# Moving the block inverses' transfers to GpSimd's queue in a hybrid decoder layer, with new transfer prices in the planner

## The chip, the core and the metric

The kernel runs on one core of one Trainium2 chip. The core has a matrix engine (TensorE, PE in the profile), a vector engine (VectorE, DVE), a scalar engine (ScalarE, ACT), a general engine (GpSimd, POOL) and a queue engine (SyncE, SP) that issues transfers. Each takes its own instructions in order and waits on semaphores for the others. Transfers between DRAM and the on-chip memory (SBUF) are issued by SP, ACT or POOL and carried out by 16 transfer engines. The metric is the device time in microseconds (us), the median of several executions; the profile is of one further execution.

## The reference

One layer of a decoder, with a residual and a last norm, in float32 (1024 tokens, width 2048):

```python
h = rmsnorm(x, ln_g);  proj = h @ w_in                     # 2048 x 6672
g_u, g_v, g_z, d_q, d_k, d_v, d_z, d_a, d_b, c_q, c_z = split(proj)
out_a = gmlp_spatial_gating(g_u, g_v, ...) * silu(g_z)     # 4 groups of 128, chunks of 128
q, k, v = split(causal_conv_silu(concat(d_q, d_k, d_v)))   # 8 heads of 128
o = gated_delta_rule(l2norm(q), l2norm(k), v, g, beta)
out_b = rmsnorm(o, dn_norm_g) * silu(d_z)
out_c = softmax(c_q @ mk.T / sqrt(128)) @ mv * silu(c_z)   # 256 memory tokens, 4 heads
y = rmsnorm(x + concat(out_a, out_b, out_c) @ w_out, final_g)
```

The delta rule solves, in every chunk and head, a triangular system with a unit diagonal, T = (I + A)^-1, where A holds the decayed products of the keys. That inverse is what the change is about.

## The kernel before, in words

Products in full precision are made from float32 split into a high and a low part: ACT makes the high part (a cast: `whi`, `ahi`, `zh`), DVE the low one (a subtraction: `wlo`, `alo`, `zl`), and PE adds three products. So each operand that comes from DRAM goes transfer, cast, subtraction, matmul. The large products use a seven-product scheme over 2 x 2 blocks (`seven`): a step takes two left and two right blocks of 128 x 512 and makes 24 matmuls of 512 columns. Three buffers hold raw left operands and three hold split ones, and likewise for the right side.

The delta rule's heads come in pairs. `front` makes a pair's keys, queries and products `gt` (128 x 1024) for one half of the tokens. `blocks_out` (L958) cuts the 32 x 32 blocks of the diagonal out of `gt` and stores them to DRAM (`gdr`), four transfers a pair, each of 256 runs of 128 bytes. When four pairs are there, `inverse` (L971) loads them (`gd`, one block per partition), with 16 transfers from POOL, and inverts all blocks at once by 31 elimination steps on DVE (62 operations, interleaved with other work). It stores the inverses `ti` (to `tdr`) and their transposes `gd` (to `udr`). `levels` (L999) later loads these 32 x 32 blocks into `tblk` and `ut`, 12 transfers of SP a pair, and builds 128 x 128 inverses from them by small matmuls, before `back` runs the scan over the chunks. This happens twice: "early" for heads 0 to 3, whose scan runs beside the first large products, and "late" for heads 4 to 7.

Before the change ACT's queue issues the stores of `gdr` (32 in all) and of `tdr` and `udr` (four each per inverse, 128 KB each); POOL issues the loads of `gd`. POOL also does the masks of the decay matrices, the small powers of the norms, and memsets.

The order of everything is written by a planner (`Plan`, L54). It records all operations with what they depend on, gives each a price, and runs a list schedule: every engine takes, of the operations that are ready, the one with the lowest rank and then the earliest in the program. `issue` (L223) then emits the operations sorted by planned time. Each engine's order in the built program is thus a consequence of the prices. For transfers the prices are the issue time on the queue, a share of a common pipe (bytes over 300 per ns, at least 512 bytes a row), a fixed latency of 1600 ns, and additions for some shapes. ACT's transfers have a pipe of their own at half the rate.

All operations are recorded through one helper, so nearly every row of the profile has the line L292 (the emitting loop); tiles tell them apart. In the built program a transfer of SP or ACT takes the next of eight semaphores, and waits for the one that used it before; POOL's transfers have eight others.

Of the kernel before, what the change touches and what calls it, by code (L numbers as in the profile page):

```python
# [44 lines left out]


class Op:
    __slots__ = ("eng", "fn", "args", "kw", "cls", "idx", "cost", "lat", "nbytes", "lock", "n", "succ", "ready", "at",
                 "lead", "tail", "table")


# [9 lines left out]
class Plan:  # L61
    SEEN = {"pe": 55.0, "act": 35.0, "dve": 35.0, "pool": 78.0, "sp": 60.0}
    SLACK = 600.0
    OVERLAP = {"pe": 0.0, "act": 90.0, "dve": 80.0, "pool": 50.0, "sp": 0.0}
    DMA_RATE = 300.0
    DMA_FIXED = 1600.0
    SWITCH = 250.0
    TABLES = {AF.Exp: "exp", AF.Silu: "silu", AF.Gelu_apprx_tanh: "gelu"}
    TABLE_LOAD = 1500.0
# [113 lines left out]
    def price(self, o, name, outs, ins):  # L183

        out = outs[0]
        n = math.prod(out.shape[1:])
        both = [*outs, *ins]
        psum = any(i.space == PSUM for i in both)
        pointer = any(i.shape[-1] == 1 and math.prod(i.shape[1:]) == 1 for i in ins[1:])
        o.nbytes = o.lock = 0  # L190
        o.lat = 0.0
        if name == "dma_start":
            o.cost = {"sp": 380.0, "act": 430.0, "pool": 1000.0}[o.eng]
            rows = math.prod(out.shape[:-1])
            o.nbytes = max(4 * math.prod(out.shape), 512 * rows)
            src = ins[0]
            pieces = src.shape[-1] < 128 or out.shape[-1] < 128
            if out.space == DRAM:
                o.lat = 9000.0 if out.shape == (32, 8, 32) else 3000.0
            elif pieces or out.shape[0] < 32:  # L200
                o.lat = 2400.0
            elif list(src.ap)[0][0] == 0:
                o.lat = 4000.0
        elif o.eng == "pe":
            passes = 1 if ins[0].dtype == F32R else 2 if name == "transpose" else 4
            o.cost = max(13.3 + n / 2.4 * passes, 222.0 if passes == 4 else 110.0) if out.shape[0] == P else 30.0
            o.lat = 175.0
        elif o.eng == "act":
            o.cost = (165.0 if psum else 200.0) + 0.82 * n + (105.0 if pointer else 0.0)
            o.cost += 190.0 if "accum_out" in o.kw else 0.0  # L210
        elif o.eng == "dve":
            n = max([n] + [math.prod(i.shape[1:]) for i in ins])
            o.cost = (n + 151) / 0.96 + (60.0 if pointer and name == "scalar_tensor_tensor" else 0.0)
            o.lock = not psum and (name.startswith("tensor_") or name == "scalar_tensor_tensor")
            o.lock = o.lock and name != "tensor_reduce"
        else:
            o.lock = 1
            if name in ("memset", "affine_select"):
                o.cost = 100.0 + 0.83 * n * (1 if name == "memset" else 1.4)
                o.lat = 800.0 if name == "affine_select" else 0.0  # L220
            else:
                o.cost = 750.0 + 150.0 * (n - 1) if n < 8 else 200.0 + 2.1 * n

    def issue(self):
        free = dict.fromkeys(self.SEEN, 0.0)
        soon = {e: [] for e in free}
        now = {e: [] for e in free}
        held = {"dve": 0.0, "pool": 0.0}
        dma = beside = 0.0
        table = "exp"  # L230
        for o in self.ops:
            if o.n == 0 and o.lead is o:
                heapq.heappush(soon[o.eng], (0.0, o.idx))
        left = len(self.ops)
        while left:
            best = None
            for e in free:
                if now[e]:
                    t = free[e]
                elif soon[e]:  # L240
                    t = max(free[e], soon[e][0][0])
                else:
                    continue
                if best is None or t < best[0]:
                    best = (t, e)
            t, e = best
            while soon[e] and soon[e][0][0] <= t:
                i = heapq.heappop(soon[e])[1]
                heapq.heappush(now[e], (self.ops[i].cls, i))
            if e == "act":  # L250
                other = [(c + self.STAY * (self.ops[i].table not in (None, table)), i, c) for c, i in now[e]]
                _, i, c = min(other)
                now[e].remove((c, i))
                heapq.heapify(now[e])
                head = self.ops[i]
            else:
                head = self.ops[heapq.heappop(now[e])[1]]
            for o in (head, *head.tail):
                t = max(t, free[e])
                if o.table not in (None, table):  # L260
                    t, table = t + self.TABLE_LOAD, o.table
                o.at = t
                left -= 1
                if o.lock:
                    t = max(t, held["pool" if e == "dve" else "dve"])
                end = t + o.cost
                if o.lock:
                    held[e] = end
                free[e] = end - min(self.OVERLAP[e], 0.5 * o.cost)
                done = end + o.lat  # L270
                if o.nbytes and e == "act":
                    beside = max(beside, end) + 2 * o.nbytes / self.DMA_RATE
                    done = beside + self.DMA_FIXED + o.lat
                elif o.nbytes:
                    dma = max(dma, end) + o.nbytes / self.DMA_RATE
                    done = dma + self.DMA_FIXED + o.lat
                for s in o.succ:
                    if s.eng != e or o.nbytes:
                        when = done + self.SEEN[s.eng] + (self.SLACK if s.eng == "pe" else 0.0)
                    elif e == "pe":  # L280
                        when = free[e]
                    else:
                        when = end + 34.0
                    s.ready = max(s.ready, when)
                    s.n -= 1
                    if s.n == 0:
                        heapq.heappush(soon[s.eng], (s.ready, s.idx))
            if len(head.tail) > 7:
                free[e] += self.SWITCH
        self.ops.sort(key=lambda o: (o.at, o.idx))  # L290
        for o in self.ops:
            o.fn(*o.args, **o.kw)  # L292
# [3 lines left out]
def kernel(  # L296
# [35 lines left out]
    def DT(shape, name, dt=F32):  # L332
        return dr.tile(list(shape), dt, name=name, tag=name)[:]
# [624 lines left out]
    def blocks_out(gt, n):  # L958

        gv = gt.rearrange("p h t i -> p (h t) i")  # L960
        gdr = [DT([8, 32, 32], f"gdr{n}_{b}") for b in range(4)]
        for b in range(4):
            sl = slice(b * 32, (b + 1) * 32)
            with rank(1):
                S.dma_start(gdr[b].rearrange("c j i -> j c i"), gv[sl, :, sl])
        return gdr

    def flat(start, *aps):
# [2 lines left out]
    def inverse(gdrs, n, cls):  # L971

        nr = 32 * len(gdrs)
        gd = ring["inv"]()[0:nr].rearrange("p (a b) -> p a b", b=32)
        for i, gdr in enumerate(gdrs):
            for b in range(4):
                with rank(1):
                    flat(G.dma_start, gd[i * 32 + b * 8 : i * 32 + (b + 1) * 8], gdr[b])
        ti = ring["inv"]()[0:nr].rearrange("p (a b) -> p a b", b=32)
        tmp = y1[0:nr].rearrange("p c m -> p (c m)")  # L980
        with rank(4):
            G.memset(ti, 0.0)
            G.affine_select(out=ti, in_=ti, compare_op=ALU.not_equal, fill=1.0, base=0,
                            pattern=[[1, 32], [-1, 32]], channel_multiplier=0)
        with rank(cls):
            for j in range(31):
                n1, m = 31 - j, j + 1
                tv = tmp[:, 0 : n1 * m].rearrange("p (n m) -> p n m", m=m)
                V.tensor_tensor(out=tv, in0=bc(gd[:, j, j + 1 :], m), in1=rep(ti[:, j, 0:m], n1), op=ALU.mult)
                V.tensor_tensor(out=ti[:, j + 1 :, 0:m], in0=ti[:, j + 1 :, 0:m], in1=tv, op=ALU.add)  # L990
            V.tensor_copy(gd.rearrange("p i m -> p m i"), ti)
        tdr, udr = ([DT([32, 32, 32], f"{t}{n}_{i}") for i in range(len(gdrs))] for t in ("tdr", "udr"))
        for i in range(len(gdrs)):
            with rank(1):
                flat(S.dma_start, tdr[i], ti[i * 32 : (i + 1) * 32])
                flat(S.dma_start, udr[i], gd[i * 32 : (i + 1) * 32])
        return list(zip(tdr, udr))

    def levels(gt, tdr, udr):  # L999

# [771 lines left out]
```

## Time and profile before

| | us |
|---|---|
| median of 3 executions | 1661.45 (1657.06 to 1662.36) |
| profiled execution | 1662.46 |
| its span, first to last instruction | 1660.7 |

The page lists, for each engine, busy time and share of the span. The list of waits names, for an engine, what ended its idle time, the sum, how often, and the longest. In a timeline a row is start, duration, engine, operation, output and inputs, count, and in brackets the idle time ahead of it and what ended it; ACTq, SPq and POOLq are issues of transfers. The row of a window gives the stretch, its length, the busy time of PE, PE's weight loads, DVE, ACT and POOL, the granted clock of PE as a share of full speed, the busy share of the transfer engines, and GB/s. A tile's row gives the shortest, median and longest duration in ns, and "to landing" the time from a transfer's issue to its arrival.

### The profile page before, as it was taken

How to read it: one execution, taken by the hardware profiler on the slowest of the kernel's cores; microseconds unless marked ns; L12 is line 12 of the kernel's file. 1: busy time of each engine (PE TensorE's matmuls, PEld its weight loads, DVE VectorE, ACT ScalarE, POOL GpSimd, SP SyncE). 2: the span in 40 equal slices, each digit the busy share in tenths (PEclk: the TensorE clock that was granted, in tenths of full speed). 3: DMA queues.
4: the chain of work that ended last, by engine and by line, in shares of the span. 5: the costliest groups of instructions: out<-in, count | busy, mean ns of one | idle time of the engine just before them, and what ended most of it. 6: DMA issues, size and time to landing. Idle time of an engine off the chain costs nothing.

```text
span 1660.7 us, 26037 instructions
## 1 busy us (share of the span) xinstructions
PE 1623.1 (98%) x8570; PEld 1357.9 (82%) x8570; DVE 1253.7 (75%) x2081; ACT 1027.4 (62%) x2226; POOL 109.2 (7%) x166
## 2 busy tenths in 40 slices
PE   8999999999899999999999998999999999999997
PEld 7888888887788888878887886888888878788886
DVE  4865777778666567989998885777768887688875
ACT  5957765765275556987775345776666774345445
POOL 0000100130000000100013000000000000000001
PEclk9999999999999999999999999999999999999999
DMA  7887888797888886599878977788968769679746
GB/s 253 241 235 222 256 288 244 231 311 269 280 270 263 283 273 201 192 283 337 294 250 274 303 230 205 232 263 305 312 209 291 264 220 353 202 251 307 227 140 241
DMA packets 320625, 427.88 MB, mean 258 GB/s; under 512 B 58669, under 2 KB 139238, under 8 KB 320490
## 3 DMA queue, kind: packets, MB, share of 16 engines
q1 hardware_dynamic: 308290, 418.87, 77.6%
q10 hardware_dynamic: 10088, 4.21, 1.0%
q0 software_dynamic: 2112, 3.15, 0.7%
q8 instruction: 67, 1.10, 0.3%
q14 instruction: 68, 0.56, 0.1%
HBM read 338.52 MB, written 87.06 MB: 256 GB/s over the span
## 4 chain that ended last, share of the span: by engine, by line
PE 82%; DMA 7%; DVE 5%; ACT 2%; issue 2%; SPq 0%; ACTq 0%; DVEq 0%; POOLq 0%; POOL 0%
PE acc L292 62%; PE dn L292 21%; DMA wraw<-in_w_in_dram 2%; DVE wlo L292 1%; DMA wraw<-hTd 1%; DMA wraw<-in_w_out_dram 1%; DVE alo L292 1%; ACT whi L292 1%; DMA y<-in_w_in_dram 1%; DVE y L292 0%; SPq L292 0%; ACTq L292 0%; DMA hTd<-tn 0%; ACT ahi L292 0%; DVE wraw L292 0%
## 5 line engine op out<-in xcount | busy, mean ns | idle before, releaser
L292 PE MATMUL acc<-ahi,whi 128*128 128x512 f32 (+1 forms) x1152 | 451.0, 392 | 1.2 <-ACT whi L292 0.9
L292 PE MATMUL acc<-alo,whi 128*128 128x512 f32 (+1 forms) x1152 | 451.0, 392 | 0.0
L292 PE MATMUL acc<-ahi,wlo 128*128 128x512 f32 (+1 forms) x1152 | 450.3, 391 | 0.2 <-DVE wlo L292 0.2
L292 PEld LDWEIGHTS acc<-ahi,whi 128*128 128x128 f32 x1152 | 217.3, 189 | 43.4 <-ACT whi L292 1.3
L292 PEld LDWEIGHTS acc<-ahi,wlo 128*128 128x128 f32 x1152 | 217.2, 189 | 41.5 <-DVE wlo L292 0.8
L292 PEld LDWEIGHTS acc<-alo,whi 128*128 128x128 f32 x1152 | 217.1, 188 | 40.7
L292 PE MATMUL acc<-ahi,zh 128*128 128x512 f32 x736 | 237.1, 399 | 6.0 <-DVE y L292 5.0
L292 DVE TENSOR_TENSOR wlo<-wraw,whi 128x512 fp32r<-128x512 f32 (+1 forms) x170 | 157.3, 926 | 73.9 <-ACT whi L292 64.5
L292 ACT CAST whi<-wraw 128x512 fp32r<-128x512 f32 (+1 forms) x170 | 137.3, 808 | 121.8 <-PE acc L292 69.1
L292 DVE TENSOR_TENSOR alo<-raws,ahi 128x1024 fp32r<-128x1024 f32 x131 | 159.7, 1220 | 51.0 <-ACT ahi L292 48.3
L292 ACT CAST ahi<-raws 128x1024 fp32r<-128x1024 f32 x131 | 137.4, 1049 | 62.2 <-PE dn L292 28.2
L292 PEld LDWEIGHTS acc<-ahi,zh 128*128 128x128 f32 x736 | 138.7, 191 | 33.9 <-ACT whi L292 5.4
L292 PE MATMUL acc<-ahi,zl 128*128 128x512 f32 x368 | 146.3, 397 | 0.0
L292 DVE TENSOR_TENSOR ahi<-y,ahi 128x1024 fp32r<-128x1024 f32 x65 | 79.2, 1218 | 34.6 <-ACT ahi L292 24.2
L292 ACT CAST ahi<-y 128x1024 fp32r<-128x1024 f32 x65 | 68.1, 1048 | 45.2 <-PE acc L292 20.3
L292 PEld LDWEIGHTS acc<-ahi,zl 128*128 128x128 f32 x368 | 70.1, 190 | 13.7
L292 ACT CAST zh<-wraw 128x1024 fp32r<-128x1024 f32 x36 | 37.8, 1050 | 42.2 <-PE acc L292 25.2
L292 DVE TENSOR_TENSOR zl<-wraw,zh 128x1024 fp32r<-128x1024 f32 x36 | 43.9, 1220 | 21.5 <-ACT zh L292 21.3
L292 PE MATMUL dn<-wlo,ahi 128*128 128x512 f32 x152 | 59.0, 389 | 0.0
L292 PE MATMUL dn<-whi,alo 128*128 128x512 f32 x152 | 59.0, 389 | 0.0
L292 PE MATMUL dn<-whi,ahi 128*128 128x512 f32 x152 | 58.8, 389 | 0.0
L292 POOL TENSOR_TENSOR small<-small,mhalf 128x1 f32<-128x1 f32 x26 | 17.1, 662 | 627.7 <-DVE small L292 627.7
(387 smaller groups left out, 3105.0 us busy)
## 6 DMA issues: line engine op xcount, KB each, us to landing
wraw<-in_w_in_dram SPq DMA_DIRECT2D x268, 256.0 KB, 4.4
raws<-sd SPq DMA_DIRECT2D x148, 256.0 KB, 4.0
y<-in_w_in_dram SPq DMA_DIRECT2D x92, 256.0 KB, 4.7
y<-sd SPq DMA_DIRECT2D x77, 256.0 KB, 4.7
wraw<-in_w_out_dram SPq DMA_DIRECT2D x64, 256.0 KB, 4.1
raws<-h0d SPq DMA_DIRECT2D x54, 256.0 KB, 5.1
y<-in_w_out_dram SPq DMA_DIRECT2D x33, 256.0 KB, 4.1
sd<-zg SPq DMA_DIRECT2D x32, 256.0 KB, 5.9
```

What stands on the lines that cost most here:

```text
L292: o.fn(*o.args, **o.kw)
```

## The change

Three things change. The stores of `gdr` in `blocks_out`, and those of `tdr` and `udr` in `inverse`, are issued by POOL (`G`) in place of ACT (`S`). `tdr` and `udr` become one DRAM tensor each per inverse, stored by one transfer of 512 KB in place of four of 128 KB; `levels` gets slices of it. The planner prices a transfer by its packets (8.5 ns and 0.0368 ns a byte each, over 16 engines), with 2900 ns of fixed latency, other issue prices, and other additions for stores to DRAM and for broadcasts. The operations on PE and DVE are the same ones; the planner writes a new order for all engines.

```diff
-    DMA_RATE = 300.0
-    DMA_FIXED = 1600.0
+    PACKET = (8.5, 0.0368)
+    QUEUES = 16
+    DMA_FIXED = 2900.0
...
-            o.cost = {"sp": 380.0, "act": 430.0, "pool": 1000.0}[o.eng]
-            rows = math.prod(out.shape[:-1])
-            o.nbytes = max(4 * math.prod(out.shape), 512 * rows)
+            o.cost = {"sp": 440.0, "act": 430.0, "pool": 700.0}[o.eng]
             src = ins[0]
-            pieces = src.shape[-1] < 128 or out.shape[-1] < 128
+            run = 4 * min(out.shape[-1], src.shape[-1])
+            fixed, byte = self.PACKET
+            o.moves = 4 * math.prod(out.shape) / run * (fixed + byte * run) / self.QUEUES
             if out.space == DRAM:
-                o.lat = 9000.0 if out.shape == (32, 8, 32) else 3000.0
-            elif pieces or out.shape[0] < 32:
-                o.lat = 2400.0
+                o.lat = 3000.0 if run < 512 else 1500.0
             elif list(src.ap)[0][0] == 0:
-                o.lat = 4000.0
+                o.lat = 3500.0
...
-                    dma = max(dma, end) + o.nbytes / self.DMA_RATE
+                    dma = max(dma, end) + o.moves
                     done = dma + self.DMA_FIXED + o.lat
...
             with rank(1):
-                S.dma_start(gdr[b].rearrange("c j i -> j c i"), gv[sl, :, sl])
+                G.dma_start(gdr[b].rearrange("c j i -> j c i"), gv[sl, :, sl])
...
-        tdr, udr = ([DT([32, 32, 32], f"{t}{n}_{i}") for i in range(len(gdrs))] for t in ("tdr", "udr"))
-        for i in range(len(gdrs)):
-            with rank(1):
-                flat(S.dma_start, tdr[i], ti[i * 32 : (i + 1) * 32])
-                flat(S.dma_start, udr[i], gd[i * 32 : (i + 1) * 32])
-        return list(zip(tdr, udr))
+        tdr, udr = (DT([nr, 32, 32], f"{t}{n}") for t in ("tdr", "udr"))
+        with rank(1):
+            flat(G.dma_start, tdr, ti)
+            flat(G.dma_start, udr, gd)
+        return [(tdr[i : i + 32], udr[i : i + 32]) for i in range(0, nr, 32)]
```

More of the change, by code (lines that the diff above doesn't have):

```diff
@@ L47 @@
 class Op:
-    __slots__ = ("eng", "fn", "args", "kw", "cls", "idx", "cost", "lat", "nbytes", "lock", "n", "succ", "ready", "at",
+    __slots__ = ("eng", "fn", "args", "kw", "cls", "idx", "cost", "lat", "moves", "lock", "n", "succ", "ready", "at",
                  "lead", "tail", "table")
@@ L189, in price @@
         pointer = any(i.shape[-1] == 1 and math.prod(i.shape[1:]) == 1 for i in ins[1:])
-        o.nbytes = o.lock = 0
+        o.moves = o.lock = 0
         o.lat = 0.0
         if name == "dma_start":
-            o.cost = {"sp": 380.0, "act": 430.0, "pool": 1000.0}[o.eng]
-            rows = math.prod(out.shape[:-1])
-            o.nbytes = max(4 * math.prod(out.shape), 512 * rows)
+            o.cost = {"sp": 440.0, "act": 430.0, "pool": 700.0}[o.eng]
             src = ins[0]
-            pieces = src.shape[-1] < 128 or out.shape[-1] < 128
+            run = 4 * min(out.shape[-1], src.shape[-1])
+            fixed, byte = self.PACKET
+            o.moves = 4 * math.prod(out.shape) / run * (fixed + byte * run) / self.QUEUES
             if out.space == DRAM:
-                o.lat = 9000.0 if out.shape == (32, 8, 32) else 3000.0
-            elif pieces or out.shape[0] < 32:
-                o.lat = 2400.0
+                o.lat = 3000.0 if run < 512 else 1500.0
             elif list(src.ap)[0][0] == 0:
-                o.lat = 4000.0
+                o.lat = 3500.0
         elif o.eng == "pe":
@@ L270, in issue @@
                 done = end + o.lat
-                if o.nbytes and e == "act":
-                    beside = max(beside, end) + 2 * o.nbytes / self.DMA_RATE
+                if o.moves and e == "act":
+                    beside = max(beside, end) + 2 * o.moves
                     done = beside + self.DMA_FIXED + o.lat
-                elif o.nbytes:
-                    dma = max(dma, end) + o.nbytes / self.DMA_RATE
+                elif o.moves:
+                    dma = max(dma, end) + o.moves
                     done = dma + self.DMA_FIXED + o.lat
                 for s in o.succ:
-                    if s.eng != e or o.nbytes:
+                    if s.eng != e or o.moves:
                         when = done + self.SEEN[s.eng] + (self.SLACK if s.eng == "pe" else 0.0)
```

## The prediction

> **What bounds the kernel now.** I read the page's head first, then who TensorE (PE) waited for, then the chain of waits and the timelines around the two longest waits.
>
> ```profile
> span 1660.7 us, 26037 instructions
> PE 1623.1 (98%) x8570; PEld 1357.9 (82%) x8570; DVE 1253.7 (75%) x2081; ACT 1027.4 (62%) x2226; POOL 109.2 (7%) x166
> ```
> PE is busy in all but 1660.7 - 1623.1 = 37.6 us, and the change leaves its instructions alone, so only those 37.6 us, and time lost to a lower clock, can be won. Who PE waited for, longest first:
>
> ```profile
> PE dn L292 <- DVE el L292: 6.8, 1, 6.8
> PE acc L292 <- DVE y L292: 5.0, 1, 5.0
> PE dn L292 <- DMA kT<-in_mem_dram: 4.2, 1, 4.2
> PE dn L292 <- DVE ai L292: 1.9, 2, 1.4
> PE acc L292 <- ACT zh L292: 1.1, 1, 1.1
> ```
> The first two, with the 1.1 us shortly behind the second, are 12.9 of the 37.6 us. Both stand behind the stores of an inverse (the lines that the change moves). ACT's timeline in the two places:
>
> ```profile
> 425.29 1.06 ACT L292 CAST zh<-wraw 128x1024 fp32r<-128x1024 f32 x1 [3.48 <-PE acc L292]
> 425.95 1.71 ACTq L292 DMA_DIRECT2D tdrearly<-inv  x3
> 428.78 5.05 ACTq L292 DMA_DIRECT2D udrearly<-inv  x3
> 435.37 0.31 ACTq L292 DMA_DIRECT2D tdrearly<-inv  x1
> 436.09 0.31 ACTq L292 DMA_DIRECT2D udrearly<-inv  x1
> 436.50 1.04 ACT L292 CAST ahi<-y 128x1024 fp32r<-128x1024 f32 x1 [10.15 <-DMA udrearly<-inv]
> ...
> 989.05 3.73 ACTq L292 DMA_DIRECT2D tdrlate<-inv  x4
> 995.51 6.34 ACTq L292 DMA_DIRECT2D udrlate<-inv  x4
> 1001.95 0.62 ACT L292 CAST whi<-kT 128x512 fp32r<-128x512 f32 x1 [12.15 <-DMA tblk<-tdrlate]
> ```
> Eight stores hold ACT's in-order queue for 10.15 and 12.15 us, though an unhindered issue takes 0.31 us. In the built program every transfer of SP and ACT also waits for the one eight places earlier, over eight semaphores that the two queues share; so each store stands for a wide load of SP to land, and the casts stand behind the stores. VectorE (DVE) and the chain show what follows:
>
> ```profile
> 425.68 0.19 DVE L292 TENSOR_TENSOR inv<-inv,y 128x31 f32<-128x31 f32 x1
> 437.57 1.22 DVE L292 TENSOR_TENSOR ahi<-y,ahi 128x1024 fp32r<-128x1024 f32 x1 [7.56 <-ACT ahi L292]
> ```
> ```profile
> 284.73 26.68 PE acc L292 x122
> 430.16 5.19 DMA wraw<-in_w_in_dram
> 435.37 3.33 DMA tdrearly<-inv
> 441.28 12.40 PE acc L292 x42
> 459.91 0.84 PE dn L292 x8
> 1009.10 2.08 PE dn L292 x8
> 1011.18 2.50 PE acc L292 x6
> ```
> No cast, so no subtraction, so no matmul until 441.28. The waits cost twice, since the granted clock falls behind each:
>
> ```profile
> 440.00:445.00 5.00, 3.72 (x9) 2.98 (x10) 5.00 (x8) 1.42 (x2) 0.00 (x0) 0.50 0.55 139
> 1010.00:1015.00 5.00, 5.00 (x47) 3.88 (x47) 3.17 (x6) 1.20 (x3) 0.61 (x2) 0.65 0.56 102
> ```
> A wide matmul takes 26.68/122 = 0.22 us at full clock. The 42 behind the early wait took 12.40 instead of 42 x 0.22 = 9.2 us: 3.2 us. Behind the late one, 2.08 - 0.84 = 1.2 us (eight dn matmuls, against the same at full clock) and 2.50 - 6 x 0.22 = 1.2 us: 2.4 us.
>
> **The change part by part.**
>
> *The 16 stores of the inverses leave ACT; four stores of 512 KB take their place on GpSimd (POOL).* ACT's stand goes, and with it PE's two waits: early 5.0 + 1.1 + 3.2 = 9.3 us, late 6.8 + 2.4 = 9.2 us, together **-18.5 us**. What is late next is the level matmuls, which need the stored blocks back. The nearest row for a 512-KB transfer on POOL is its load of the memory keys, for the blocks themselves the layout loads on SP:
>
> ```profile
> L292 POOL DMA_DIRECT2D gt<-kvd x2: 745/745/745, 1093.3 to 1153.5; - x2
> DMA to landing us min/median/max: 4.0/5.7/6.6
> ```
> ```profile
> 439.19 3.05 SPq L292 DMA_DIRECT2D tblk<-tdrearly  x6
> ```
> ```profile
> L292 ACTq DMA_DIRECT2D tdrearly<-inv x4: 308/314/433, 425.9 to 435.4; - x4
> DMA to landing us min/median/max: 1.8/3.5/6.6
> ```
> From the last elimination to the first level matmul: 0.1 to the issue, 5.7 until it has landed, five block loads at 3.05/6 = 0.5, i.e. 2.5, and 3.5 for the last to land: 11.8 us (0.1 + 6.6 + 2.5 + 6.6 = 15.8 with the longest landings). What covers it is read from the built order. The products run in steps of 24 wide matmuls (5.3 us), and a step's operand can be split only when the step three before is over. The early elimination now ends behind split 7 (split 8 before), the level matmuls stand 49 wide matmuls earlier than before; so 55 to 79 matmuls, 12.1 to 17.4 us, lie between: a wait of 0, at worst 15.8 - 12.1 = 3.7 us. The late one ends behind split 89 (95 before), and the levels stand 154 matmuls earlier: 45 to 69 matmuls, 9.9 to 15.2 us, lie between: 0 to 1.9 us, at worst 5.9. I take 1.0 and 1.5: **+2.5 us**.
>
> The page "DMA: Bandwidth & Descriptors" of the Trainium skill (section "Anatomy of one DMA — SWDGE (gpsimd) path") puts a GpSimd transfer at about 2.0 us plus its bytes at 436 GB/s; for 512 KB that is an estimate of 3.2 us, with which both waits would be nought and the time 2.5 us less. The measured 5.7 us of a loaded queue decides here.
>
> *The 32 stores of the blocks move from ACT to POOL.*
>
> ```profile
> L292 ACTq DMA_DIRECT2D gdr<-gt x32: 309/469/2578, 187.2 to 888.9; - x32
> L292 POOL DMA_DIRECT2D inv<-gdr x32: 518/518/717, 353.3 to 901.1; - x32
> ```
> ACT is rid of 32 x 0.47 = 15 us, at 62% busy and with PE not waiting there: 0. On POOL a store of 256 rows of 128 bytes is nearest to the 745 ns of the 256-row load (518 ns for 8 rows is the low end): 32 x 0.745 = 24 us on an engine busy 109 of 1661 us: 0. Behind them in POOL's queue stand the masks of the next head and small powers:
>
> ```profile
> POOL E L292 <- ACT vs L292: 265.2, 16, 83.1
> ```
> POOL stood 265.2/16 = 17 us on average ahead of each mask, which hides four stores (3.0 us); without that cover a mask, and the head behind it, would come 3.0 us later. A pair's four stores wait for its last product, as they did on ACT.
>
> The stores of the last pair lie on the path to the elimination: 3.0 us of stores, then landing and loads in one queue. In the new order the late elimination starts 82 to 106 matmuls (18 to 23 us) behind the last pair's products. I work the chain at 3.0 + 5.3 (the block stores' median landing, from the last row of this part) + 15 loads at 0.52 (7.8), of which some 3 us run before that landing, + 5.4 for the last: about 18.5 us. That just fits.
>
> ```profile
> DMA to landing us min/median/max: 2.2/5.3/9.7
> ```
>
> *The schedule's prices.* The same instructions stand on PE, DVE and SP in another order from the start: a wide transfer's price in the plan's pipe falls (2-KB packets, 128 x (8.5 + 0.0368 x 2048)/16 = 671 ns, not 874), its fixed latency grows by 1.3 us. This is no work, only other places to wait. At the good end it removes half of what PE idles outside the two places, the start and the end: some 5 us; at the bad end it adds as many waits as the 4.2-us one as there are inverses, 8 us. A plan that expects 3.6 us where such a load takes 4.4 (row below) should lose less than one that expects 2.5; a redrawn order also meets new collisions. I take **+2.0**.
>
> ```profile
> wraw<-in_w_in_dram SPq DMA_DIRECT2D x268, 256.0 KB, 4.4
> ```
>
> *SP* now shares no semaphore with ACT's stores, but its layout loads stand for the 512-KB store. In the new order 20 of them are issued in one run at both inverses (20 x 0.5 = 10 us without a wide load; before, six and twelve with a store between). Hidden by the four steps whose operands are loaded ahead of the run and by the scan's matmuls between them; in matmul time 40 us lie from step 6 to step 12: 0, and the price of the cover being gone is the third rival.
>
> Sum: -18.5 + 2.5 + 2.0 = -14.0 us; span 1660.7 - 14.0 = 1646.7. The profiled execution took 1662.46 us, 1.76 over its span, and stands 1.01 over the median of 1661.45: 1646.7 + 1.76 - 1.01 = **1647.5 us**.
>
> **The rivals.**
>
> 1. *One wait comes back* (chance 0.14). The late elimination's inputs have about 18.5 us and 18 to 23 of cover. 5 us more of landing (the 9.7 of the row above instead of 5.3) stops DVE in its order, PE waits about 5 us at the levels and pays 2.4 for the clock: 1647.5 + 7.4 = 1655.
> 2. *The change doesn't do what it says* (0.08): ACT's stand only hid that the loads were late, and PE waits for them instead: no gain, 1661. For it: the transfer engines were full while ACT stood (the row below, 1.00 and 340 GB/s). Against it: once ACT was free the casts ran back to back, so their data was there.
> ```profile
> 430.00:435.00 5.00, 5.00 (x23) 4.13 (x22) 0.01 (x1) 0.00 (x0) 0.00 (x0) 1.00 1.00 340
> ```
> 3. *Slower* (0.18): the run of layout loads on SP. SP stands about 5.8 us for the store, issues for 10 us, and only then takes the next wide loads: 5.8 + 10 + two or three loads (1.5) + 4.4 landing + cast and subtraction (1.04 + 1.22) = 24 us. The four loaded steps are 96 x 0.22 = 21 us plus what the scan puts between. If the scan's matmuls are late too, the cover ends and the ring of buffers refills from empty: 10 us of queue plus 5 us of clock and refill at each inverse, 1647.5 + 2 x 13 = 1674. It ends slower than before from 7 us a place on (half of the 14.0).
> 4. *POOL's issues wait for DVE* (0.05). If each store of the last pair and of the inverse waited for one 1.2-us subtraction, each inverse would come 4 x 1.2 + 1.2 = 6 us later, with about 2.8 of clock: 1647.5 + 2 x 8.8 = 1665. The even 518 ns of 32 POOL issues, beside a DVE that is 75% busy, speaks against it. By the page "SBUF — State Buffer" of the Trainium skill (section "SBUF: two separate sides") GpSimd can't write its descriptors while DVE holds the port that the two share, so that its transfers starve; the trace of before doesn't bear that out.
>
> **How the numbers follow.** The forecast (1640 to 1655, its own range) has 0.55; the rivals 0.14, 0.08, 0.18 and 0.05. About 0.3% (5 us) is what a measurement of this kernel can tell from no change: faster is below 1656.5: 0.55 and most of the first rival, 0.68. Within: the second and fourth and a rest, 0.14. Slower: 0.18. The range goes from 1638 (the sum without the 4.5 us of new waits and a further 5 us won by the order) to 1666, just past the fourth rival; the third stays out.
>
> **What would show it.** Right: no ACT cast waits over 5 us behind an inverse; PE's list of waits holds none over 4 us but the first load; the clock shows no half-speed stretch between the first 100 us and the end; POOL's block stores take 0.6 to 0.9 us, the 512-KB stores land in 4 to 7. Wrong: PE waits at the level matmuls (tblk) or for a wide load (wlo, alo) behind the run of layout loads; DVE standing at the first elimination for POOL's loads; POOL issues of 2 us; waits of 3 us or more in new places, which would be the redrawn order.

## The result and the profile after

The changed kernel takes 1655.26 us in the median (1651.73 to 1659.28, 18 executions) against 1661.41 (1657.06 to 1666.81, 18 executions) for the kernel before: the ratio is 0.996, with a 95% interval of 0.9949 to 0.997. It is faster by some 6 us, less than half of the 14 us that were forecast. (Two line numbers above are off: in the kernel before, `Plan` begins at L61 and `issue` at L224.)

The head of the page after, for the same two rows as shown of before:

```profile
span 1652.2 us, 26083 instructions
PE 1621.7 (98%) x8570; PEld 1357.8 (82%) x8570; DVE 1259.4 (76%) x2081; ACT 1036.5 (63%) x2226; POOL 128.4 (8%) x202
```

The span fell by 8.5 us: TensorE (PE) idles 1652.2 - 1621.7 = 30.5 us instead of 37.6, and its busy time, in which the lower clock is paid, fell by 1.4. PE's list of waits after, longest first (who PE waited for: sum in us, how often, longest):

```profile
PE dn L291 <- DMA y<-in_mem_norm_g_dram: 4.3, 1, 4.3
PE dn L291 <- DMA tn<-vd: 3.0, 1, 3.0
PE dn L291 <- DVE steps L291: 2.3, 2, 2.1
PE dn L291 <- issue: 2.2, 2, 1.8
PE dn L291 <- ACT steps L291: 1.9, 1, 1.9
PE dn L291 <- DMA el<-vd: 1.7, 1, 1.7
```

The first is the first load of the kernel. The two long waits of before, 6.8 and 5.0 us, are gone. But most of the next five, 11.1 us together, stand where the two long ones stood: 3.7 us at the early inverse (the 1.8 of "issue" at 428.8 us, ahead of the first level matmul, and the 1.9 at 445.9), 6.8 at the late one (976 to 1008 us). SP's timeline shows what fills its queue at the early one (start, duration, transfer, count):

```profile
424.35 4.27 SPq L291 DMA_DIRECT2D tblk<-tdrearly  x5
429.06 2.25 SPq L291 DMA_DIRECT2D ut<-udrearly  x4
431.36 0.44 SPq L291 DMA_DIRECT2D tblk<-tdrearly  x1
431.85 3.92 SPq L291 DMA_DIRECT2D ut<-udrearly  x8
435.87 0.84 SPq L291 DMA_DIRECT2D tblk<-tdrearly  x2
436.81 1.36 SPq L291 DMA_DIRECT2D pd<-y  x3
438.26 1.55 SPq L291 DMA_DIRECT2D wraw<-in_w_in_dram  x3
```

Twenty layout loads take SP 12.4 us (424.35 to 436.71), 3.7 of which it stands for earlier wide loads to land, and no wide load goes out before 438.26. At the late inverse the first twenty take 12.0 us (954.06 to 966.10). VectorE (DVE) and ScalarE (ACT) show who was short of it:

```profile
443.18 1.33 DVE L291 TENSOR_TENSOR y<-y,wraw 128x512 f32<-128x512 f32 x2 [4.94 <-DMA wraw<-in_w_in_dram]
446.51 1.05 ACT L291 CAST whi<-wraw 128x1024 fp32r<-128x1024 f32 x1 [2.84 <-DVE wraw L291]
447.46 0.27 ACT L291 ACTIVATE steps<-dn 128x128 f32<-128x128 f32 x1
```

DVE stood 4.94 us for a wide load, ACT's cast stood for DVE, and behind the cast in ACT's in-order queue was the copy of `steps` that PE stood for from 445.9. At the late inverse PE waits for the scan's own inputs, which SP loads, and for a `steps` of DVE behind a product that stood 2.97 us for a wide load:

```profile
975.21 0.43 SPq L291 DMA_DIRECT2D el<-vd  x1
1002.94 0.39 SPq L291 DMA_DIRECT2D tn<-vd  x1
```

The granted clock (the column behind POOL's) fell in three places among these waits:

```profile
430.00:435.00 5.00, 4.41 (x86) 3.31 (x86) 2.54 (x4) 0.73 (x2) 0.61 (x2) 0.66 0.34 53
445.00:450.00 5.00, 3.10 (x14) 2.37 (x12) 3.26 (x5) 2.99 (x7) 0.00 (x0) 0.81 1.04 340
1005.00:1010.00 5.00, 2.04 (x10) 1.73 (x9) 2.53 (x3) 0.00 (x0) 0.00 (x0) 0.79 0.98 301
```

So the question is whether the queue brought what was forecast and the new order lost it, and by what.

### The profile page after: what moved, and what is told of

Its sections match the earlier page's. It is cut to its first block, busy times and chain, and to the rows that moved or that the text cites. A ratio compares the mean times of both kernels' runs of the same rounds, so it can differ in the third digit from the quotient of the medians.

```text
span 1652.2 us, 26083 instructions
## 1 busy us (share of the span) xinstructions
PE 1621.7 (98%) x8570; PEld 1357.8 (82%) x8570; DVE 1259.4 (76%) x2081; ACT 1036.5 (63%) x2226; POOL 128.4 (8%) x202
## 4 chain that ended last, share of the span: by engine, by line
PE 87%; DMA 7%; DVE 2%; SPq 1%; ACT 1%; issue 1%; POOLq 0%; POOL 0%; DVEq 0%; ACTq 0%
PE acc L291 67%; PE dn L291 20%; DMA wraw<-in_w_in_dram 2%; SPq L291 1%; DMA raws<-sd 1%; DMA y<-in_w_in_dram 1%; DMA xr<-pd 1%; DMA kT<-in_mem_dram 1%; DMA qT<-in_w_in_dram 1%; DMA mixd<-y 0%; DVE wlo L291 0%; DMA tn<-vd 0%; DMA E<-in_gmlp_ws_dram 0%; DVE alo L291 0%; ACT whi L291 0%
```

## The experiments

Each kernel is compared with the kernel before on the same chip; a difference between two kernels is that of their ratios, times 1661.4 us. Two kinds of kernel occur: some keep an order that is already there, instruction for instruction, and change only which queue issues some transfers (the planner runs first, then the emitting loop swaps the issuing function); in the others the planner draws a new order.

### The queue alone, at the order of before

```diff
+        for o in self.moved:              # in issue(), after the sort
+            o.fn = self.pool.ns.dma_start
...
-                S.dma_start(gdr[b]...)
+                R.moved.append(S.dma_start(gdr[b]...))
...
+                R.moved.append(flat(S.dma_start, tdr[i], ...))
+                R.moved.append(flat(S.dma_start, udr[i], ...))
```

> The plan and the order of the kernel before on every engine, with the 48 stores of the blocks and inverses issued by GpSimd instead of ScalarE at the same place of the order (still four of 128 KB for each layout). Theory Q (ScalarE's stand cost the whole 18 us, and the redrawn order gave most of it back, with the level matmuls pulled forward and the layout loads in one run): 1661 - 16 = about 1645 us, PE's waits of 5.0 and 6.8 us gone. Theory S (SyncE's queue, with its layout loads, holds PE whoever issues the stores): 1655 us, waits of 5 to 7 us in sum at each inverse. Theory P (what was gained comes from the order that the new prices draw, at the start and between the inverses): 1658 us or more.

Measured: 1648.83 us (1646.34 to 1652.83), ratio 0.9922 (0.9909 to 0.9934): 13 us less than before, between theory Q's 1645 and theory S's 1655 and nearer to Q. ACT's timeline at the early inverse has no stand for stores any more:

```profile
424.96 1.05 ACT L295 CAST ahi<-y 128x1024 fp32r<-128x1024 f32 x1
429.67 1.05 ACT L295 CAST ahi<-raws 128x1024 fp32r<-128x1024 f32 x1 [3.66 <-issue]
```

What stays there is one PE wait of 3.1 us for a cast of `zh` at 455 us, with a half-speed stretch behind it. The move by itself does most of what the prediction said of it.

### Only the sixteen stores of the inverses

The same edit for `tdr` and `udr` alone; the 32 stores of `gdr` stay with ACT.

```diff
+                R.moved.append(flat(S.dma_start, tdr[i], ...))
+                R.moved.append(flat(S.dma_start, udr[i], ...))
```

> As the first, but only the 16 stores of the inverses go to GpSimd; the 32 block stores stay on ScalarE. Theory Q: within 2 us of the first, about 1646, since the block stores stand in no path of PE. If it lies over 3 us above the first, the block stores on ScalarE cost something that no wait of PE showed. Theory S: 1655 to 1656. Theory P: 1658 or more.

Measured: 1650.07 us (1646.99 to 1653.59), ratio 0.9931 (0.9917 to 0.9945). The intervals of the two overlap: the inverses' stores carry nearly all of the gain, and the block stores cost and bring nothing that shows.

### The prices alone, and the queue with the old prices

The first takes the new prices into the kernel before and leaves the stores on ACT, the second takes the new queue and the joined stores with the old prices. In both the planner draws its own order.

```diff
-    DMA_RATE = 300.0
-    DMA_FIXED = 1600.0
+    PACKET = (8.5, 0.0368)
+    QUEUES = 16
+    DMA_FIXED = 2900.0
```

> The new prices with the queues and the separate stores of before; the plan draws its own order. Theory Q: ScalarE stands behind both inverses as before: 1658 to 1664 us. Theory P: 1655 us, the changed kernel's time, with ScalarE's stand still there at a place where it costs less. Theory S: 1660.

> The transfers moved and joined as in the changed kernel, planned with the old prices (GpSimd's issue at 1000 ns, 1600 ns of fixed latency); the plan draws its own order. Theory Q: between 1645 and 1652, the queue's gain less what this order takes. Theory S: 1655. Theory P: 1658 or more, as the new order's gains at the start and between the inverses are missing.

Measured: 1680.88 us, ratio 1.0116 (1.0103 to 1.0129), for the prices alone; 1684.82 us, ratio 1.0144 (1.0129 to 1.0158), for the queue with old prices. Both halves of the change, drawn by themselves, are slower than before by 19 and 24 us, though together they are faster. No theory foresaw this: theory P's "1658 or more" takes the second in, but speaks of gains that go missing, not of a loss. In the first kernel ACT still stands for its stores (a copy waits 10.68 us at 412 to 423 us, and PE 7.2 us for it), as theory Q said. The second has the transfers of the run "Both, at the order of before" below (ratio 0.991) and differs from it in the order alone, so its order costs (1.0144 - 0.991) x 1661.4 = 39 us. Its waits, longest first:

```profile
PE dn L292 <- ACT vs L292: 10.2, 8, 2.9
PE dn L292 <- DVE steps L292: 7.7, 3, 6.2
```

They stand at 1225 to 1275 us, where the last scan was left without wide matmuls beside it; at the two inverses (from 440 and 1067 us on, each for 100 us) PE waits for nothing. So the order that the planner draws has a spread of its own, as large as anything the transfers do. Which operation tipped it stays open.

### Fewer stores, left on ACT

At the order of before; the eight stores of an inverse become two of 512 KB, still issued by ACT.

```diff
+        for parts, whole in self.joined:  # in issue(), after the sort
+            parts[0].args = whole         # one store of 128 x 1024
+            for o in parts[1:]:
+                o.fn = lambda *a: None
```

> The order of the kernel before, instruction for instruction on PE, DVE, GpSimd and SP; the sixteen 128-KB stores of tdr and udr become four of 512 KB and stay on ScalarE's queue, as do the stores of gdr. Theory 'count' (ScalarE stands some 1.3 us for each store, about 9 us behind eight): two stores would hold it 3 us at most, so PE's waits and the half-speed stretches at the two inverses go and the time is 1648 to 1651, that of the queue moved alone. Theory 'queue' (any store in ScalarE's queue makes the casts behind it stand until the other queues let it go, however few stores): a cast wait of 5 us or more stays behind the stores and the time is 1653 to 1660.

Measured: 1650.75 us (1647.4 to 1652.99), ratio 0.993 (0.9914 to 0.9947). ACT's timeline at the early inverse:

```profile
427.98 0.35 ACTq L301 DMA_DIRECT2D tdrearly<-inv  x1
429.09 0.34 ACTq L301 DMA_DIRECT2D udrearly<-inv  x1
429.56 1.05 ACT L301 CAST ahi<-y 128x1024 fp32r<-128x1024 f32 x1 [1.29 <-DVE inv L301]
```

With two stores the cast behind them stands 1.29 us instead of 10.15, and for DVE, which makes the second store's data. The theory "count" holds: the same bytes in fewer stores don't hold the queue, and joining the stores removes the stand as well as moving them does. Either half would have done; together they don't add up by more than the intervals.

### Both, at the order of before

All stores in GpSimd's queue and joined: the change without its prices and so without a new order.

> The order of the kernel before; all inverse stores in GpSimd's queue and tdr and udr in one transfer each: the change without its new prices and so without a redrawn order. Theory that the redrawn order alone took the rest of the gain: 1647 to 1651, the same as the queue moved alone (1648.8). Rival, that joining costs (all parts must wait for the whole and 512 KB land later than 128): 1652 to 1656, with PE waiting 2 us or more for tblk or ut at the level matmuls.

Measured: 1647.48 us (1646.17 to 1648.91), ratio 0.991 (0.9896 to 0.9925), 15.0 us less than before. Its head:

```profile
span 1647.2 us, 26039 instructions
PE 1618.8 (98%) x8570; PEld 1356.1 (82%) x8570; DVE 1255.3 (76%) x2081; ACT 1030.3 (63%) x2226; POOL 128.3 (8%) x202
```

PE idles 28.4 us and is busy 4.3 us less than before. Joining costs nothing that shows. The rest of the change, the new order, therefore gave back (0.996 - 0.991) x 1661.4 = 8.3 us, with some 3 us either way by the intervals. SP has a long run of layout loads here too, 18 in 11 us at the early inverse:

```profile
434.01 4.24 SPq L303 DMA_DIRECT2D tblk<-tdrearly  x6
439.32 5.73 SPq L303 DMA_DIRECT2D ut<-udrearly  x12
```

### The layout loads off SP, at both orders

At the order of before (with the stores as in the run above), and at the order of the changed kernel, the 96 layout loads go to GpSimd's queue.

```diff
         def blocks_in(dst, src, b, e=slice(0, NB)):
-            Q.dma_start(dst, ...)
+            R.moved.append(Q.dma_start(dst, ...))
```

> As the run before, and the loads of the layouts (tblk and ut, 96 issues) also in GpSimd's queue instead of SP's. Theory that SP's run of layout loads delays the wide weight loads behind it: the wait for zh of 3.1 us at the early inverse and its half-speed stretch (3.4 us) go, 1642 to 1646. Rival, that the transfers themselves fill the DMA engines there: 1647 to 1650, the same waits under other names. Second rival: GpSimd's 96 issues of some 0.5 us reach tblk later than SP does and PE waits for tblk: 1651 or more.

> The changed kernel's order, with its layout loads (tblk and ut) in GpSimd's queue. Theory that SP's run in front of the wide loads makes the three waits left at each inverse (5.1 and 6.8 us): 1648 to 1651. Rival, that the redrawn order itself (which work is put beside the level matmuls) makes them: 1653 to 1657, no change.

Measured at the order of before: 1646.54 us, ratio 0.9908 (0.9891 to 0.9924), against 0.991 with the loads on SP: no difference that shows. What the theory named did happen, the wait for `zh` fell from 2.8 to 1.1 us and the half-speed stretch behind it went, but its time (1642 to 1646) was not reached. At the changed kernel's order: 1643.16 us (1641.81 to 1646.04), ratio 0.9887 (0.987 to 0.9904), which is 12.1 us under the changed kernel (some 3 us either way) with not one instruction moved on PE, DVE or ACT. That is more than the theory's 1648 to 1651. Its head, the longest two of PE's waits, and the windows that answer to the three above:

```profile
span 1641.6 us, 26113 instructions
PE 1617.5 (99%) x8570; PEld 1353.9 (82%) x8570; DVE 1258.5 (77%) x2081; ACT 1033.7 (63%) x2226; POOL 182.0 (11%) x298
```
```profile
PE dn L294 <- DMA y<-in_mem_norm_g_dram: 3.8, 1, 3.8
PE dn L294 <- DVE ai L294: 1.9, 1, 1.9
```
```profile
430.00:435.00 5.00, 4.77 (x93) 3.41 (x92) 3.13 (x5) 1.74 (x6) 4.57 (x9) 1.00 0.68 200
445.00:450.00 5.00, 5.00 (x104) 4.01 (x103) 3.00 (x8) 2.20 (x9) 1.66 (x4) 1.00 1.05 379
1005.00:1010.00 5.00, 5.00 (x24) 4.14 (x23) 3.50 (x8) 2.43 (x7) 1.01 (x1) 1.00 1.03 388
```

The waits at both inverses are gone or under 1 us, and the clock stays at 1.00. The span is 10.6 us shorter, of which 6.4 are idle time (30.5 to 24.1) and 4.2 are busy time (1621.7 to 1617.5), which with the same instructions on PE is the price of the clock. GpSimd's timeline at the early inverse, and the row of SP's first wide loads behind it:

```profile
417.10 0.76 POOL L294 DMA_DIRECT2D tdrearly<-inv  x1 [22.72 <-DVE inv L294]
...
424.18 2.82 POOL L294 DMA_DIRECT2D tblk<-tdrearly  x5 [5.60 <-DMA tdrearly<-inv]
426.99 1.74 POOL L294 DMA_DIRECT2D ut<-udrearly  x3
```
```profile
433.31 1.32 SPq L294 DMA_DIRECT2D wraw<-in_w_in_dram  x3
```

The wide loads go out at 433.31 instead of 438.26. The rival, that the redrawn order makes the waits whoever loads, falls: with the loads off SP the new order is no slower, 0.9887 against 0.9908, or 3.5 us less (the intervals overlap). But the loads on SP don't cost by themselves either, since at the order of before moving them brought nothing that shows. The loss needs both: SP's layout loads, and an order that puts small operands of PE behind them.

### One inverse at a time

The changed kernel's order; only the 48 loads of the early inverse, or only those of the late one, go to GpSimd.

```diff
-            Q.dma_start(dst, ...)
+            o = Q.dma_start(dst, ...)
+            if any(src is a for a in R.chosen):   # the slices of one inverse
+                R.moved.append(o)
```

> The changed kernel's order; only the 48 layout loads of the early inverse go to GpSimd's queue, those of the late one stay with SP. With all 96 moved the time fell from 1655 to 1643. Theory that SP's run of loads costs the same kind of wait at each inverse: about half the gain, 1648 to 1651, with the waits for tblk at 429 us and steps at 446 us and their two half-speed stretches gone and those for el, ut and tn at 976 to 1008 us still there. Rival, that the late run makes nearly all of it (its three waits are the longer, 6.8 against 5.1 us): 1652 to 1655.

> The counterpart: only the 48 layout loads of the late inverse go to GpSimd's queue. Theory of equal waits: 1647 to 1650, with the waits of 1.7, 2.1 and 3.0 us at 976 to 1008 us and the half-speed stretch there gone. Rival, that the early run makes nearly all (it has two half-speed stretches, the late one): 1652 to 1655. If the parts add up, this gain and that of the early loads alone sum to 12 us.

Measured: early 1646.59 us (1645.58 to 1650.57), ratio 0.9904 (0.9887 to 0.9922), 9.3 us less than the changed kernel; late 1650.13 us (1646.69 to 1650.98), ratio 0.9918 (0.9903 to 0.9934), 7.0 us less. Early alone came out a little below its theory's range and late alone just above its own; the sum, 16.3, is above the 12.1 of both moved, by no more than the four intervals allow. PE's waits tell that each cures its own place, for the first kernel and then the second:

```profile
PE dn L295 <- DMA el<-vd: 1.9, 1, 1.9
PE dn L295 <- DVE steps L295: 1.8, 2, 1.5
```
```profile
PE dn L295 <- ACT steps L295: 4.1, 1, 4.1
PE dn L295 <- issue: 1.7, 1, 1.7
```

With the early loads moved, the wait for `el` and a `steps` of the late place stay; with the late ones moved, the `steps` of the early place stays. But the place that was left alone didn't stay as it was. In the first kernel the late waits sum to 4.4 us instead of 6.8, without a half-speed stretch. In the second the early `steps` is 4.1 us instead of 1.9, and the half-speed stretch behind it 10.2 us instead of 3.4, though up to there its transfers and queues are those of the changed kernel. A profile is one execution, and the waits at one place differed here by some 2 us from one to the next; so how the gain divides between the two places stays open.

### Only the loads of the transposes

The changed kernel's order; the 48 loads of `ut` go to GpSimd, those of `tblk` stay with SP.

```diff
-            Q.dma_start(dst, ...)
+            o = Q.dma_start(dst, ...)
+            if src is udr:
+                R.moved.append(o)
```

> The changed kernel's order; of each inverse's layout loads only those of ut (the transposes, 48 of 96) go to GpSimd's queue, those of tblk stay with SP. Theory 'behind' (the length of SP's run keeps back the wide loads after it): the run of 20 falls to 8, the wide loads go out some 6 us earlier, 1644 to 1648, and what stays is a wait for tblk of about 2 us. Theory 'itself' (the blocks that the first level matmul needs come late from a queue that stands for its own earlier transfers): the wait for tblk and its half-speed stretch stay, 1650 to 1655.

Measured: 1647.17 us (1644.83 to 1650.35), ratio 0.9908 (0.9891 to 0.9925), 8.6 us less than the changed kernel, inside the range of "behind". But the place looks like both theories. SP's run of what is left:

```profile
426.01 9.61 SPq L294 DMA_DIRECT2D tblk<-tdrearly  x8
```
```profile
PE dn L294 <- issue: 3.2, 1, 3.2
```

Eight loads hold SP for 9.61 us, 1.2 us each, where GpSimd issued five in 2.82: SP's run isn't issue time alone, it stands for earlier transfers as ACT did (5.8 of the 9.61 us by its list of waits: 1.8 each for a `wraw` and a `tblk`, 1.4 for `y`, 0.8 for `raws`). The wait ahead of the first level matmul stays (3.2 us), as "itself" said; the later waits at both inverses are gone or shorter, as "behind" said. So of the 12.1 us some 8.6 go with the loads of `ut`; the rest, with those of `tblk`, is within the intervals.

### The loads planned on GpSimd

The changed kernel with the queue of the layout loads given to the planner, which draws a new order.

```diff
-            Q.dma_start(dst, src[b * NB : (b + 1) * NB][e].rearrange("c i j -> i c j"))
+            G.dma_start(dst, src[b * NB : (b + 1) * NB][e].rearrange("c i j -> i c j"))
```

> The changed kernel with the layout loads given to GpSimd before the planner runs, so that it also writes a new order of all engines for it. If the price of such a move is only the queue's, the time is that of the same move at a fixed order, 1641 to 1646. If what a redrawn order brings is as wide as the draws so far (-4 with the loads off SP, +19 and +23 in the two orders drawn by the prices alone and by the queue alone), it lies anywhere from 1638 to 1668, and what PE idles outside the start, the end and the inverses (2.5 us in the changed kernel) tells it.

Measured: 1640.67 us (1640.23 to 1642.29), ratio 0.9868 (0.985 to 0.9886): faster than both kernels, 15.3 us under the changed one, and at the low end of what was expected of the queue alone (1641 to 1646). Its head:

```profile
span 1638.5 us, 26118 instructions
PE 1615.8 (99%) x8570; PEld 1353.7 (83%) x8570; DVE 1258.9 (77%) x2081; ACT 1032.7 (63%) x2226; POOL 182.6 (11%) x298
```

PE idles 22.7 us, of which some 15 lie at the start and the end. This draw of the order was a good one, 3 us better than the fixed order with the same loads moved, within the intervals.

## Why the prediction was wrong

**ACT's stand (-18.5): right in kind, and 3.5 us too large.** The same edit at the order of before measured -15.0, and there neither inverse shows a wait for `tblk` or `ut`. The stand was per store (10.15 us for eight, 1.29 for two), and the wait cost twice (9.2 us of idle time and 4.3 of clock against 12.9 and 5.6 forecast). What the forecast missed is the wait of 2.8 us for `zh` that is left at the early inverse, with a half-speed stretch of 3.4 us. That the block stores cost nothing held: they took 0.58 to 0.78 us where "What would show it" asked for 0.6 to 0.9, and the loads beside them are as before:

```profile
L291 POOL DMA_DIRECT2D gdr<-gt x32: 584/584/784, 182.9 to 859.1; - x32
L291 POOL DMA_DIRECT2D inv<-gdr x32: 499/511/583, 349.1 to 869.5; - x32
```

**The new waits at the level matmuls (+2.5): about right.** They were worked out for the new order. There the first level matmul of the early inverse waits 1.8 us and that of the late one not at all, against 1.0 and 1.5. The chain from the last elimination took 15.3 us (415.26 to 430.59), not 11.8: the store landed after 6.5 us instead of 5.7, and SP needed 4.3 us instead of 2.5 for the five block loads. The half-speed stretch behind the wait was not in the sum.

**SP's layout loads, put at 0: this is the step that failed.** In the new order they cost 12.1 us, the 1.8 and its stretch included. The prediction counted a run of 20 at 10 us (12.4 in the trace) and said that the four steps loaded ahead of it and the scan's matmuls between, 40 us, hide it. The cover was counted in wide matmuls, and none of the waits named is for a wide matmul's operand: PE waited for the first level matmul's blocks, for the scan's own inputs behind layout loads in SP's queue (`el`, `tn`), and for small results (`steps`) that stood in ACT's or DVE's queue behind work without data. The runs moved all 96 loads and not the runs of 20 alone: `tn` went out 37 us after the late run had ended, with twelve more layout loads between. So which of the loads cost how much stays open.

The third rival named nearly this mechanism, with a price of 13 us a place (its own terms, 10 and 5, make 15) on condition that the scan's matmuls are late too; they were. Measured singly the places cost 9.3 and 7.0 us, together 12.1, so it was the rival's mechanism at about half its price. Its stand of 5.8 us for the store didn't come: the store had landed by 422.3, and SP's last wait before 424.35 was for a wide load.

**The redrawn order, put at +2.0 between -5 and +8.** This term and the 0 for SP's loads measured +8.3 together. With the loads off SP the new order is worth -3.5 us, inside the range and not clear of zero. That the bad end happens to equal the 8.3 us is luck: it was worked out from other waits. And the order drawn with the old prices, at +39, shows that the bounds were far too narrow for what such a planner can do.

Step by step from kernel to kernel the ratios read -15.0 us for the stores, -0.3 for the loads moved at the order of before, -3.5 for the new order, +12.1 for the loads back on SP. Since each step starts where the last one ended, the sum must come to the whole change (0.996, or -6.6); it tests nothing.

**The rivals.** The first gave the right time, 1655, by the wrong way: DVE stood 1.6 us for its inputs at the late elimination, not 5, and PE's late waits are for `el`, `tn` and `steps`.

```profile
DVE y L291 <- DMA inv<-gdr: 1.6, 1, 1.6
```

The second falls with the queue alone (0.9922). The fourth falls at its price: by the 584 and 511 ns of the rows above, no block store waited for a subtraction of 1.2 us, beside a DVE that is 76% busy. But its mechanism is in the traces, in one place. DVE's copy of `inv`, which makes the transposes and had no transfer of GpSimd beside it before the change, now runs beside the first 512-KB store:

```profile
415.30 1.14 DVE L291 COPY inv<-inv 128x1024 f32<-128x1024 f32 x1
415.82 0.74 POOL L291 DMA_DIRECT2D tdrearly<-inv  x1 [23.08 <-DVE inv L291]
```

The store's issue ends 0.12 us after the copy. In all traces in which the two overlap, nine at the early inverse and five at the late one, it ends 0.11 to 0.13 us after the copy; in the late ones it takes 1.46 to 1.48 us (1.48 in the kernel with the loads moved), against 0.54 for the store of `udr` and 0.64 for the late store here, which ended before the copy began. The Trainium skill's page "SBUF — State Buffer" (section "SBUF: two separate sides") describes this: GpSimd can't write its descriptors while DVE runs certain operations, a float32 copy among them. The trace agrees for the copy, and shows no such stand beside the subtractions.

**What would show it.** No cast stood behind an inverse's store, as said. No wait of PE was over 4 us but the first, as said, and yet it was a poor sign: many short waits took the place of two long ones. The half-speed stretches did not go (three of 3.4 us at the inverses where there had been two of 6.8), and that was the sign that counted. The issues on GpSimd held, and the four 512-KB stores landed in 4.2 to 7.5 us, where 4 to 7 was said.

## What to carry to other kernels

In this program an in-order queue that issues transfers paid per transfer, and by its waits it paid for the landing of earlier ones: fewer or elsewhere helped equally, and once was enough. When one queue is relieved, look at the next run of small transfers in another queue and ask what stands behind its last one, down to the small operand of a small matmul; a cover counted in the large operation hides nothing from that. Where a planner redraws the whole order, fix the order and change one thing, since its draws alone ranged here from -3.5 to +39 us.

## What the runs showed of the hardware

Moving 96 small loads from SP to GpSimd, between the same instructions, was worth 12.1 us at one order and nothing that shows at another. By the Trainium skill's page "DMA: Bandwidth & Descriptors" (section "Issuing engines are not separate DMA queues") a second issuing engine saves only the issuing sequencer's time, "usually small relative to the DMA itself". That agrees in kind, and not in size: the queue was held 12.4 us by 20 loads (0.62 each; 3.7 us of it standing for earlier transfers), against a landing of 4.3 us for a wide load (the row of the transfers' view of the changed kernel below), and 1.2 us by each where only `tblk` was left.

```profile
wraw<-in_w_in_dram SPq DMA_DIRECT2D x268, 256.0 KB, 4.3
```

The half-speed stretch at 431 us began after a wait of 1.8 us, that at 448 after one of 1.9, that at 1007.5 within one of 3.0. The Trainium skill's page "TensorE: Matmul & The Clock Gate" (Part 1) lets the clock fall after an idle window of about 3.4 us. Here less idle time was enough, with small matmuls around it (86 in the five microseconds from 430, where 23 wide ones fill as many), though waits of the same length, 1.7 and 2.1 us at 976 and 986 us, left the clock alone. What tells them apart stays open.

The 512-KB stores on GpSimd took longer than forecast at the early inverse. In the changed kernel they landed 6.5 and 7.5 us after their issue there, and 5.4 and 4.2 at the late one; the prediction took 5.7, and its estimate by the Trainium skill's page "DMA: Bandwidth & Descriptors" was 3.2. The 5.7 is not the median of the row that the prediction shows above it, but of all twelve transfers of `kvd`; the two loads of that row landed in 4.1, and GpSimd's two other loads of 512 KB in 5.7.
